# A hybrid DeltaNet and state-space layer on one Trainium2 core: values ahead of gates, the DeltaNet gate amid the state-space scan, and its branch projection in plain float32 at the scan's end

## The chip, the core and the metric

The kernel runs on one core of one Trainium2 chip. The core has a matrix engine (PE; its weight loads are shown as PEld), a vector engine (DVE), a scalar engine (ACT), a general engine (POOL) and 16 DMA engines; most DMAs are issued by SP's queue, the stores of results by ACT's. On-chip data lie in SBUF; matmuls write to PSUM, eight banks in all.

The metric is device microseconds (us) of one execution. Before the change the median of three runs is 1307.09 us (1301.83 to 1307.75). The profile is of one more execution.

## The reference, cut to what matters

One layer over 256 latent tokens and 256 context tokens with 1024 channels, everything in float32: a half-step SwiGLU block, a token mixer, a second half-step SwiGLU block and a final norm. The mixer is where the change lies. It projects its normalised input `h` with one wide weight, and runs a gated DeltaNet and a Mamba-2 scan (SSD) in both directions beside each other; each branch is gated, projected to 1024 channels, scaled by a sigmoid gate, and the sum is projected once more:

```python
u = h @ w_in
qkv, za, a, beta, zb, xbc, dt, gates = jnp.split(u, ...)
qkv = jax.nn.silu(conv(qkv, gdn_conv_w))          # q, k, v: 8 heads of 128
...
a_mat = jnp.where(strict, jnp.einsum('bnhid,bnhjd->bnhij', kb, k) * decay, 0.0) + jnp.eye(CHUNK)
sol = lax.linalg.triangular_solve(a_mat, rhs, left_side=True, lower=True, unit_diagonal=True)
...
ya = rmsnorm(o, gdn_norm_g) * jax.nn.silu(za)
yb = rmsnorm((y + mb_d * xs) * jax.nn.silu(zb), mb_norm_g)
merged = jax.nn.sigmoid(ga) * (ya @ w_branch_gdn) + jax.nn.sigmoid(gb) * (yb @ w_branch_mb)
return merged @ w_out
```

Here `o` is the DeltaNet's output, `y` the scan's, `ga` and `gb` the two halves of `gates`.

## The kernel before

**Tiling.** Activations stand channel-major: 128 channels on the partitions, tokens along the row, 256 for the latents alone or 512 with the context. A weight comes in units of 128 by 1024 (512 KB), one DMA each on SP's queue into one of four `raw` slots.

**Two kinds of projection.** `unit` (line 185) splits a weight into a rounded high part `whi` (ACT, line 197) and a rest `wlo` (DVE, line 201); `mm3` then runs three matmuls per block, high by high, high by low and low by high (lines 212 to 214). So go keys, values, queries, x and both branch projections. `whole` (line 634) leaves the weight as it is, and the matmul takes plain float32: so go the gates `wg` and the DeltaNet's `zA` (both line 648), and the scan's `zB` (line 1161).

**What sets the order.** The mixer's parts are generators or functions, and the string `PLAN` calls them in turn: `13/dts` sets a priority and emits `dts`, `g5` takes five steps of the gates' generator. A scheduler then orders each engine's instructions from priorities, data and free buffers by a simulated time line. So a shift in `PLAN`, or in who asks for a buffer first, moves instructions on all engines, and from then on each engine runs its list in that order.

**Keys to first merge.** `keys` (line 943) takes key heads through convolution, norm and transposes, and stores each head's Gram matrix (`pg`, line 960) to DRAM (`Gsd`); every two heads the blocks come back as `N` (line 969) in another layout. `dts` (line 870) makes the scan's step sizes and their cumulated sums `gc`, transposes these (`prow`, line 914) and stores them as `asd`. `elim` (line 1041) inverts all 32 by 32 blocks at once, on DVE, in 30 dependent steps, stores them (`Tsd`, `Ttd`), and `merge` (line 1187) loads them for one pair of token tiles and joins them with small matmuls (`pTw`, line 1242, first). Beside all this PE runs values (`values`, line 1071: projection, convolution `cv` at lines 665 to 672 on ACT and DVE, transposes `ptm`, store `vsc`), gates and queries.

**The DeltaNet chain and the scan.** After the merges, `chain_step` walks the token tiles; `gdn_norm` (line 1373) leaves `o` token-major and normalised. The scan goes by quarters (two groups of two halves). For each, `ssd_off` (line 1437) loads `xlat` and multiplies it into `yg` (line 1451), runs `pyo` and adds it (lines 1467, 1468), and `ssd_diag` (line 1471) builds two decay matrices `Es` for every token tile on DVE (lines 1499, 1507, 1510, 1512), multiplies them with x on PE (`pyd`, line 1515) and adds that (line 1516). `ssd_gate` and `ssd_norm` (lines 1518, 1527) multiply by the gate `zt`, which zB's units have stored, and scale.

**The scan's end.** `gdn_out` (line 1386) transposes `o` to channels (`pya`), multiplies by norm gain and gate (`ya`, line 1401), splits the result (`yaH` on ACT, `yaL` on POOL) and projects it with `wbg`. `ssd_out` (line 1559), for each of the two groups, transposes `yg` into PSUM (`pyb`, line 1570), one bank, and splits it (`ybH`, `ybL`, lines 1574, 1575). `mb_out` (line 1578) projects that with `wbm` (16 units), adds the branches, and projects the sum. The pools that matter: 16 slots `s4` of 4 KB per partition, shared by `yg`, `xlat`, `yaH`, `yaL`, `ybH`, `ybL`; PSUM tags `mm` (2 banks), `ch` (2), `mg` (2), `tr` (1), `sd` (1).

Of the kernel before, what the change touches and what calls it, by code (L numbers as in the profile page):

```python
# [27 lines left out]
TAGS = dict(tA=4, tS=3, tL=2, tM=2, tZ=2)  # L28
T4 = 2
NCV = 2  # L30
PLAN = """10/k3 block_decay k6 18/g5 13/dts 20/v2 g3 row_scale 5/elim 20/g7 v7 21/gdn_rows 13/m0 14/m1 13/chain_start s0 s1 m2 m3 22/q9
    B_part 27/x17 25/lat_h 22/C_part 30/g17 chain_out 13/s2 s3 14/gdn_norm 15/ssd_pre 30/zB1 zA9 zB4 15/h40 51/y0 gdn_out y1 70/mb_out"""
NG = 5
GQ = 0
EST = ("t4", "tt")
# [2 lines left out]
OSQ, YAL = "c4", "gggg"  # L38
# [30 lines left out]
ZT = ("mm", "ch")  # L69
# [67 lines left out]
class Kernel:  # L137
# [537 lines left out]
    def mixer(self, hg):  # L675
# [194 lines left out]
    def dts(self):  # L870

        nc, V = self.nc, self.nc.vector
        C = self.const
        mm = nc.tensor.matmul
        x = self.t2([P, 4, 64], "dtx", tag="tZ")
        e = self.t2([P, 4, 64], "dte", tag="tZ")
        z2 = self.t2([P, 4, 64], "dtz", tag="tL")
        V.tensor_copy(x, self.xdt)
        dt = self.dt = self.xdt
        self.softplus(dt, e, z2, x)  # L880
        g = self.t2([P, 4, 64], "dtg", tag="tL")
        V.tensor_tensor(g, dt, self.alog[:, 16:80].rearrange("p (o c) -> p o c", o=1).to_broadcast([P, 4, 64]), op=ALU.mult)
        pc = self.smp([P, 2, 4, 64], "pcd", "mg")
        for d, tri in enumerate((self.UT, self.LT)):
            mm(pc[:, 0, :, 32 * d:32 * d + 32], tri, g[:, :, 32 * d:32 * d + 32], start=True, stop=True)
        mm(pc[:, 1], self.ones, g, start=True, stop=True)
        gc = self.gc = C([P, 4, 64], "gc")
        V.tensor_copy(gc, pc[:, 0])

        gt = pc[:, 1]  # L890
        wc = self.wc = C([P, 2, 2, 32], "wc")
        for j in range(2):
            for d in range(2):
                t = 2 + j
                cs = slice(32 * d, 32 * d + 32)
                w = wc[:, j, d]
                V.tensor_tensor(w, gt[:, t, cs], gc[:, t, cs], op=ALU.subtract)
                if d == j:
                    V.tensor_tensor(w, w, gt[:, 5 - t, cs], op=ALU.add)
        nc.scalar.activation(wc, wc, AF.Exp)  # L900
        wf = wc.rearrange("p a b c -> p a (b c)")
        V.tensor_tensor(wf, wf, dt[:, 2:4], op=ALU.mult)

        wl, egm = self.wl, self.egm = C([P, 2, 32], "wl"), C([P, 2, 32], "egm")
        for d in range(2):
            cs = slice(32 * d, 32 * d + 32)
            V.tensor_tensor(wl[:, d], gt[:, d, cs], gc[:, d, cs], op=ALU.subtract)
            V.tensor_copy(egm[:, d], gt[:, d, cs])
        nc.scalar.activation(wl, wl, AF.Exp)
        nc.scalar.activation(egm, egm, AF.Exp)  # L910
        for d in range(2):
            V.tensor_tensor(wl[:, d], wl[:, d], dt[:, d, 32 * d:32 * d + 32], op=ALU.mult)
        pr = self.smp([P, P], "prow", "mg")
        nc.tensor.transpose(pr, gc[:, 0:2].rearrange("p t c -> p (t c)"), self.ident)
        rw = self.t2([P, P], "rows_a", tag="tL")
        nc.scalar.activation(rw, pr, AF.Copy, scale=-1.0)
        nc.scalar.dma_start(self.asd, rw)
# [465 lines left out]
        for t in range(2):  # L1383
            V.tensor_tensor(o[t], o[t], bc(rs[:, t], 8, P), op=ALU.mult)

    def gdn_out(self):

        nc, V = self.nc, self.nc.vector
        o, bc = self.o, self.bc
        yH = Ks(self, 8, NL, "yaH")  # L1390
        yL = Ks(self, 8, NL, "yaL")
        for h2 in range(4):
            pv = self.smp([P, 2, NL], "pya", "ch")
            for j in range(2):
# [6 lines left out]
            V.scalar_tensor_tensor(out=ya, in0=pv, scalar=self.gng, in1=zA, op0=ALU.mult, op1=ALU.mult)
            nc.scalar.copy(yH.t[j][:, hs], ya)
            (V if YAL[h2] == "v" else nc.gpsimd).tensor_tensor(yL.t[j][:, hs], ya, yH.t[j].bitcast(F32)[:, hs], op=ALU.subtract)
# [155 lines left out]
    def ssd_out(self, gi):  # L1559

        nc, V = self.nc, self.nc.vector
        y = [self.yx[gi, hf][0] for hf in range(2)]
        yH = Ks(self, 8, NL, f"ybH{gi}")
        yL = Ks(self, 8, NL, f"ybL{gi}")
        for c2 in range(4):
            pv = self.smp([P, 2, NL], "pyb", "tr")
            for j in range(2):
                c = 2 * c2 + j
                for t in range(2):
                    nc.tensor.transpose(pv[:, j, t * P:t * P + P], y[c // 4][:, t, (c % 4) * P:(c % 4) * P + P], self.ident)  # L1570
            for j in range(2):
                c = 2 * c2 + j
                g = self.mbg[:, 8 * gi + c:8 * gi + c + 1]
                nc.scalar.activation(yH[c], pv[:, j], AF.Identity, scale=g)
                V.scalar_tensor_tensor(out=yL[c], in0=pv[:, j], scalar=g, in1=yH[c].bitcast(F32), op0=ALU.mult, op1=ALU.subtract)
        self.yb.append((yH, yL))
# [124 lines left out]
```

## Time and profile before

| what | us |
|---|---|
| median of three runs | 1307.09 |
| the profiled execution's own time | 1309.47 |
| its span, first to last instruction | 1307.8 |
| first block and key units, up to 459 | PE busy 454.43 of 459 |
| rest of keys, elimination, to the first merge, 459 to 612 | PE busy 134.71 of 153 |
| merges, chain, queries and x, 612 to 855 | PE busy 236.85 of 243 |
| scan, zA, zB, 855 to 991 | PE busy 134.41, DVE 105.32 of 136 |
| scan's end and first branch, 991 to 1036 | PE busy 35.42 of 45 |
| second branch, 1036 to 1082 | PE busy 45.19 of 46 |
| output projection, second block, final norm, from 1082 | PE busy 216.78 of 226 |

The stretches are cut where the work changes. "Busy" counts an engine's instructions; the granted clock (1 is full speed) says how fast PE ran them. Its mean over the span is 0.973. A row of the chain of waits gives start, length, engine and work on the chain that ended last; a group row gives line, engine, operation, tiles and shapes with a count, then busy time and mean length in ns of one, then the engine's idle time ahead of it and what ended that.

### The profile page before, as it was taken

The numbers are of one execution on the slowest core, as the hardware profiler recorded it, in microseconds if no ns is written. First come the engines' busy times: TensorE is split into PE (matmuls) and PEld (weight loads), VectorE is DVE, ScalarE is ACT, GpSimd is POOL, SyncE is SP. The second block draws the span as 40 slices with busy tenths as digits, with TensorE's granted clock in tenths as the row PEclk, the third lists the DMA queues.
The fourth block names the chain that finished last, engine by engine and source line by source line (L and its number), as shares of the span: only waits on it lengthen the run. The fifth ranks groups of instructions, "written<-read, shape, count | busy, mean of one in ns | idle before, by whom it ended". The sixth has DMA issues, their size and how long they took to land.

```text
span 1307.8 us, 21034 instructions
## 1 busy us (share of the span) xinstructions
PE 1257.8 (96%) x8042; PEld 1096.2 (84%) x8042; DVE 950.8 (73%) x1748; ACT 482.2 (37%) x919; POOL 96.7 (7%) x119
## 2 busy tenths in 40 slices
PE   9999999999999989987999999999997999999997
PEld 8888888888899878877888899868555999999997
DVE  5997686556568964897669799847896566856655
ACT  4322122212236652254323445421223445633333
POOL 1000000000010131001110211100211002000000
PEclk9999999999999999998889999999987999999998
DMA  9566467547532389648434356568645665655552
GB/s 367 183 212 206 129 221 230 192 147 238 181 123 89 105 220 232 212 145 235 108 103 117 122 177 196 175 194 286 219 168 199 193 201 182 192 192 185 186 179 79
DMA packets 138131, 239.40 MB, mean 183 GB/s; under 512 B 41072, under 2 KB 81456, under 8 KB 137904
## 3 DMA queue, kind: packets, MB, share of 16 engines
q1 hardware_dynamic: 98688, 214.32, 51.5%
q10 hardware_dynamic: 39344, 23.76, 6.1%
q8 instruction: 63, 1.03, 0.3%
q14 instruction: 36, 0.29, 0.1%
HBM read 211.72 MB, written 26.31 MB: 182 GB/s over the span
## 4 chain that ended last, share of the span: by engine, by line
PE 65%; issue 16%; DVE 9%; DMA 8%; ACT 1%; SPq 0%; POOL 0%; ACTq 0%; DVEq 0%; POOLq 0%
PE acc L213 16%; PE acc L212 16%; PE acc L214 16%; PE acc L648 4%; DVE Es L1499 1%; PE pSs L1125 1%; PE acc L1161 1%; PE pada L318 1%; DMA raw<-in_wgs 1%; DVE Es L1510 1%; DVE wlo L201 1%; PE pn L1339 1%; DMA zsc<-zbt 1%; PE pP L1330 1%; DMA Lm<-Gsd 1%
## 5 line engine op out<-in xcount | busy, mean ns | idle before, releaser
L197 ACT CAST whi<-raw 128x1024 fp32r<-128x1024 f32 (+1 forms) x208 | 214.5, 1034 | 460.3 <-PE acc L213 350.8
L213 PE MATMUL acc<-hL,whi 128*128 128x512 f32 (+1 forms) x976 | 346.1, 355 | 0.5 <-DVE hL L468 0.5
L214 PE MATMUL acc<-hH,wlo 128*128 128x512 f32 (+1 forms) x976 | 346.5, 355 | 0.0
L212 PE MATMUL acc<-hH,whi 128*128 128x512 f32 (+1 forms) x976 | 342.4, 357 | 0.8 <-ACT cv L665 0.5
L201 DVE TENSOR_TENSOR wlo<-raw,whi 128x1024 fp32r<-128x1024 f32 (+1 forms) x208 | 249.7, 1202 | 80.0 <-ACT whi L197 78.8
L212 PEld LDWEIGHTS acc<-hH,whi 128*128 128x128 f32 x976 | 187.7, 193 | 24.6 <-ACT cv L665 0.7
L213 PEld LDWEIGHTS acc<-hL,whi 128*128 128x128 f32 x976 | 188.1, 193 | 23.9 <-DVE hL L468 0.9
L214 PEld LDWEIGHTS acc<-hH,wlo 128*128 128x128 f32 x976 | 188.0, 193 | 23.4
L290 DVE CUSTOM_DVE_ANT_0 junk<-wadat,cs 128x1024 f32<-128x1024 f32 x80 | 97.7, 1221 | 44.1 <-DMA wadat<-in_wadaT 43.4
L213 PE MATMUL acc<-aL,whi 128*128 128x256 f32 (+1 forms) x384 | 122.9, 323 | 0.0
L214 PE MATMUL acc<-aH,wlo 128*128 128x256 f32 (+1 forms) x384 | 122.3, 323 | 0.0
L212 PE MATMUL acc<-aH,whi 128*128 128x256 f32 (+1 forms) x384 | 122.2, 323 | 0.0
L667 DVE SCALAR_TENSOR_TENSOR cv<-cbuf,cc,cv 128x512 f32<-128x512 f32 (+1 forms) x144 | 97.5, 688 | 16.8 <-ACT cv L665 15.4
L648 PE MATMUL acc<-hF,raw 128*128 128x256 f32 x416 | 97.2, 390 | 7.0 <-ACT gth L1183 7.0
L648 PEld LDWEIGHTS acc<-hF,raw 128*128 128x128 f32 x416 | 80.7, 197 | 21.0 <-ACT gth L1183 7.6
L213 PEld LDWEIGHTS acc<-aL,whi 128*128 128x128 f32 x384 | 73.0, 190 | 5.6
L214 PEld LDWEIGHTS acc<-aH,wlo 128*128 128x128 f32 x384 | 72.7, 190 | 5.6
L212 PEld LDWEIGHTS acc<-aH,whi 128*128 128x128 f32 x384 | 72.6, 190 | 5.7
L604 DVE SCALAR_TENSOR_TENSOR xl<-acc,hg,xl 128x256 f32<-128x256 f32 x64 | 30.3, 481 | 47.6 <-PE acc L214 47.0
L1161 PE MATMUL acc<-raw,hF 128*128 128x512 f32 x128 | 58.6, 610 | 0.0
L1161 PEld LDWEIGHTS acc<-raw,hF 128*128 128x128 f32 x128 | 24.9, 197 | 30.0 <-issue 29.9
L401 POOL TENSOR_TENSOR sqa<-sqa,sqb 128x256 f32<-128x256 f32 x12 | 11.7, 978 | 454.9 <-ACT sqb L399 451.9
(403 smaller groups left out, 1968.4 us busy)
## 6 DMA issues: line engine op xcount, KB each, us to landing
raw<-in_wgu SPq DMA_DIRECT2D x76, 512.0 KB, 4.2
wadat<-in_wadaT SPq DMA_DIRECT2D x56, 512.0 KB, 4.1
raw<-in_wdn SPq DMA_DIRECT2D x44, 512.0 KB, 3.8
wada<-in_wada SPq DMA_DIRECT2D x16, 512.0 KB, 9.6
raw<-in_wg SPq DMA_DIRECT2D x16, 512.0 KB, 3.7
Es<-asd SPq DMA_DIRECT2D x16, 512.0 KB, 4.7
raw<-in_wxs SPq DMA_DIRECT2D x16, 512.0 KB, 4.3
raw<-in_wzB SPq DMA_DIRECT2D x16, 512.0 KB, 3.8
```

The costliest lines, as they stand in the source:

```text
L197: nc.scalar.copy(hi, raw)
L201: engs[i % len(engs)].tensor_tensor(lo[:, c:c + w], raw[:, c:c + w], hi[:, c:c + w].bitcast(F32), op=ALU.subtract)
L212: mm(acc, wh, xh, start=start, stop=False)
L213: mm(acc, wh, xl, start=False, stop=False)
L214: mm(acc, wl, xh, start=False, stop=stop)
L290: self.nc.vector.tensor_tensor_reduce(out=self.junk, in0=w, in1=self.cs[s], scale=1.0, scalar=0.0, op0=ALU.mult, op1=ALU.add, accum_out=out)
L318: mm = lambda c, q: nc.tensor.matmul(pa[:, c], loads[k][c][:, q * P:q * P + P], self.cTs[:, q:q + 1].to_broadcast([P, P // 2, 2]), start=q ...
L604: nc.vector.scalar_tensor_tensor(out=xs, in0=acc[:, NL * s - g0:NL * s - g0 + NL], scalar=hg[s][:, m:m + 1], in1=xs, op0=ALU.mult, op1=ALU ...
L648: self.nc.tensor.matmul(acc, w[:, k * P:k * P + P], self.hF[:, k], start=k == 0, stop=k == KD - 1)
L667: nc.vector.scalar_tensor_tensor(out=u3, in0=buf[:, 0:R, j:j + 64], scalar=cw[:, j:j + 1], in1=u3, op0=ALU.mult, op1=ALU.add)
L1125: nc.tensor.matmul(pS[:, d], self.Btok[:, j, m // 8], w[:, d, j], start=j == 0, stop=j == 1)
L1161: nc.tensor.matmul(accs[t], self.hF[:, k, sl], w[:, wsl], start=k == 0, stop=k == 7)
```

## The change

Four edits, beside what the scheduler makes of them.

1. In `PLAN`, three values stand where five gates stood, two gates follow behind `dts`, and the rest of the gates go ahead of the rest of the values behind the elimination.
2. `dts` loses its last four statements, which become `dts_rows` and are called behind `gdn_rows`.
3. `gdn_out` is cut in two. `gdn_pre` (transposes, gate, now into one plain float32 tile set `ya`) is called behind the last zA unit, ahead of the scan's loop and of the zB units. `gdn_out`, the projection, is called behind both `ssd_out`; its weights are taken whole, in plain float32, so no split of `ya` and none of `wbg` is left. Its accumulators alternate between two PSUM tags.
4. `pyb` alternates between the banks `tr` and `sd`.

```diff
-PLAN = """10/k3 block_decay k6 18/g5 13/dts 20/v2 g3 row_scale 5/elim 20/g7 v7 21/gdn_rows 13/m0 14/m1 ...
-    ... 15/ssd_pre 30/zB1 zA9 zB4 15/h40 51/y0 gdn_out y1 70/mb_out"""
+PLAN = """10/k3 block_decay k6 18/v3 13/dts 18/g2 20/v2 g3 row_scale 5/elim 20/g10 v4 21/gdn_rows dts_rows 13/m0 14/m1 ...
+    ... 15/ssd_pre 30/zB1 zA9 29/gdn_pre 30/zB4 15/h40 51/y0 y1 60/gdn_out 70/mb_out"""
...
+    def dts_rows(self):
+
+        nc = self.nc
         pr = self.smp([P, P], "prow", "mg")
-        nc.tensor.transpose(pr, gc[:, 0:2].rearrange("p t c -> p (t c)"), self.ident)
+        nc.tensor.transpose(pr, self.gc[:, 0:2].rearrange("p t c -> p (t c)"), self.ident)
...
-    def gdn_out(self):
+    def gdn_pre(self):
...
-        yH = Ks(self, 8, NL, "yaH")
-        yL = Ks(self, 8, NL, "yaL")
+        self.ya = Ks(self, 8, NL, "ya", F32)
         for h2 in range(4):
...
-            V.scalar_tensor_tensor(out=ya, in0=pv, scalar=self.gng, in1=zA, op0=ALU.mult, op1=ALU.mult)
-            nc.scalar.copy(yH.t[j][:, hs], ya)
-            (V if YAL[h2] == "v" else nc.gpsimd).tensor_tensor(yL.t[j][:, hs], ya, yH.t[j].bitcast(F32)[:, hs], op=ALU.subtract)
+            V.scalar_tensor_tensor(out=self.ya.t[j][:, hs], in0=pv, scalar=self.gng, in1=zA, op0=ALU.mult, op1=ALU.mult)
+
+    def gdn_out(self):
...
         for m in range(8):
-            acc = self.proj("wbg", m, yH, yL, NL)
+            w = self.whole(self.I["wbg"][m])
+            acc = self.mmp([P, NL]) if ZT[m % 2] == "mm" else self.smp([P, NL], "acc", ZT[m % 2])
+            for k in range(8):
+                nc.tensor.matmul(acc, w[:, k * P:k * P + P], self.ya[k], start=k == 0, stop=k == 7)
...
-            pv = self.smp([P, 2, NL], "pyb", "tr")
+            pv = self.smp([P, 2, NL], "pyb", ("tr", "sd")[c2 % 2])
```

What the scheduler makes of it is read from each engine's list (line, operation, tiles, shape, count of like rows). First PE at the end of the keys: `pg` are Gram matrices, `l2b` and `l2t` the norm's transposes, `pcd` the sums of `dts`; L648 is a gate, 8 matmuls a unit, L212 to L214 here a value. Before, from the last but one Gram:

```order
L960 MATMUL pg<-kT 128x128 x4
L939 MATMUL l2b<-ident,l2n 128x128 x4
L925 MATMUL l2t<-ident,kcv_3441 128x128 x2
L648 MATMUL acc<-hF,raw 128x256 x9
L914 MATMUL prow<-ident,gc 128x128
L960 MATMUL pg<-kT 128x128 x4
L939 MATMUL l2b<-ident,l2n 128x128 x4
L1000 MATMUL prow<-ident,sel_3364 128x128
L648 MATMUL acc<-hF,raw 128x256 x8
```

Now, from the third Gram ahead of the last to the one before the last (line numbers are 4 higher):

```order
L648 MATMUL acc<-hF,raw 128x256 x2
L964 MATMUL pg<-kT 128x128 x4
L943 MATMUL l2b<-ident,l2n 128x128 x4
L648 MATMUL acc<-hF,raw 128x256 x6
L885 MATMUL pcd<-dtg,UT 128x4x32
L885 MATMUL pcd<-dtg,LT 128x4x32
L886 MATMUL pcd<-dtg,ones 128x256
L214 MATMUL acc<-hH_3181,wlo 128x512
L212 MATMUL acc<-hH_3181,whi 128x512
L213 MATMUL acc<-hL_3183,whi 128x512
L214 MATMUL acc<-hH_3181,wlo 128x512
L964 MATMUL pg<-kT 128x128 x4
```

Where gates filled PE between Grams, values now do: ahead of the last Gram stand 3.4 values and two gates, where there were 1.3 values and five gates. The transpose of `dts` (L914) has left this place; it follows the third gate. Further on, the first merge (`pTw`) stands behind the first query unit and a part of it, where it stood behind six: five query projections earlier.

Second, PE at the scan's end. L1161 (now L1165) is zB, L1515 (L1522) is `pyd`, L1413 the new projection. Before:

```order
L1161 MATMUL acc<-raw,hF 128x512
L1515 MATMUL pyd<-xlat,Es 128x64 x16
L1161 MATMUL acc<-raw,hF 128x512 x23
L1515 MATMUL pyd<-xlat,Es 128x64 x16
L1396 MATMUL pya<-ident,o_7186 128x128
L1396 MATMUL pya<-ident,o_7187 128x128
```

Now:

```order
L1165 MATMUL acc<-raw,hF 128x512
L1413 MATMUL acc<-ya,raw 128x256 x2
L1522 MATMUL pyd<-xlat,Es 128x64 x16
L1413 MATMUL acc<-ya,raw 128x256 x30
L1522 MATMUL pyd<-xlat,Es 128x64 x16
L1577 MATMUL pyb<-ident,yg 128x128 x32
L1413 MATMUL acc<-ya,raw 128x256 x32
L212 MATMUL acc<-ybH_8376,whi 128x256
```

The zB units are done ahead of the last two `pyd`, half of the branch projection fills the place between these, all 32 transposes of the scan's output follow, then the other half, then `mb_out` with nothing among it. The 16 `pya` transposes now stand among the last zA unit's rows.

Third, DVE in the scan's first half. `zbt` and `zth` are the gates of zB and zA, `yg<-xlat` is the product of line 1451 (now 1458). Before, ahead of the first quarter's decay matrices:

```order
L1165 SCALAR_TENSOR_TENSOR zbt<-zbt,acc 128x512 x2
L1451 TENSOR_TENSOR yg<-xlat,mbD 128x512 x2
L1467 TENSOR_TENSOR yo<-pyo,cbm 128x512
L1128 TENSOR_TENSOR sst<-pSs,egm 128x256
L1468 TENSOR_TENSOR yg<-yg,yo 128x512
L1175 SCALAR_TENSOR_TENSOR zth<-zth,acc 128x256 x2
```

Now, behind the first quarter's decay matrices:

```order
L1179 SCALAR_TENSOR_TENSOR zth<-zth,acc 128x256
L1403 SCALAR_TENSOR_TENSOR ya<-pya,cc,zA 128x512
L1458 TENSOR_TENSOR yg<-xlat,mbD 128x512 x2
L1403 SCALAR_TENSOR_TENSOR ya<-pya,cc,zA 128x512
L1475 TENSOR_TENSOR yg<-yg,yo 128x512 x3
L1474 TENSOR_TENSOR yo<-pyo,cbm 128x512
L1458 TENSOR_TENSOR yg<-xlat,mbD 128x512 x2
L1475 TENSOR_TENSOR yg<-yg,yo 128x512
```

The products of all four quarters, and the loads of `xlat` on SP's queue ahead of them, come only behind or among the four `ya`; before, they stood among the chain's end and the x units. On SP, two of the four `zA` loads now stand among zB's weights.

More of the change, by code (lines that the diff above doesn't have):

```diff
@@ L30 @@
 NCV = 2
-PLAN = """10/k3 block_decay k6 18/g5 13/dts 20/v2 g3 row_scale 5/elim 20/g7 v7 21/gdn_rows 13/m0 14/m1 13/chain_start s0 s1 m2 m3 22/q9
-    B_part 27/x17 25/lat_h 22/C_part 30/g17 chain_out 13/s2 s3 14/gdn_norm 15/ssd_pre 30/zB1 zA9 zB4 15/h40 51/y0 gdn_out y1 70/mb_out"""
+PLAN = """10/k3 block_decay k6 18/v3 13/dts 18/g2 20/v2 g3 row_scale 5/elim 20/g10 v4 21/gdn_rows dts_rows 13/m0 14/m1 13/chain_start s0 s1 m2 m3 22/q9
+    B_part 27/x17 25/lat_h 22/C_part 30/g17 chain_out 13/s2 s3 14/gdn_norm 15/ssd_pre 30/zB1 zA9 29/gdn_pre 30/zB4 15/h40 51/y0 y1 60/gdn_out 70/mb_out"""
 NG = 5
@@ L1396, in gdn_out @@
                     nc.tensor.transpose(pv[:, j, t * P:t * P + P], o[t][:, 2 * h2 + j], self.ident)
-            ya = self.t2([P, 2, NL], "ya")
             j, hs = h2 // 2, slice(2 * (h2 % 2), 2 * (h2 % 2) + 2)
@@ L1400, in gdn_out @@
             nc.sync.dma_start(zA, self.zAsc[2 * h2:2 * h2 + 2].rearrange("m p n -> p m n"))
-            V.scalar_tensor_tensor(out=ya, in0=pv, scalar=self.gng, in1=zA, op0=ALU.mult, op1=ALU.mult)
-            nc.scalar.copy(yH.t[j][:, hs], ya)
-            (V if YAL[h2] == "v" else nc.gpsimd).tensor_tensor(yL.t[j][:, hs], ya, yH.t[j].bitcast(F32)[:, hs], op=ALU.subtract)
+            V.scalar_tensor_tensor(out=self.ya.t[j][:, hs], in0=pv, scalar=self.gng, in1=zA, op0=ALU.mult, op1=ALU.mult)
+    def gdn_out(self):
+        nc, V = self.nc, self.nc.vector
         mg = self.mg = Ks(self, 8, NL, "mg", F32)
         for m in range(8):
-            acc = self.proj("wbg", m, yH, yL, NL)
+            w = self.whole(self.I["wbg"][m])
+            acc = self.mmp([P, NL]) if ZT[m % 2] == "mm" else self.smp([P, NL], "acc", ZT[m % 2])
+            for k in range(8):
+                nc.tensor.matmul(acc, w[:, k * P:k * P + P], self.ya[k], start=k == 0, stop=k == 7)
             ga = self.t2([P, NL], "ga", tag="tL")
```

## The prediction

> **What bounds the kernel now.** I read the page's busy shares first, then the table by stretches of the span, then the chain of waits in the stretches that the change touches.
>
> ```profile
> PE 1257.8 (96%) x8042; PEld 1096.2 (84%) x8042; DVE 950.8 (73%) x1748; ACT 482.2 (37%) x919; POOL 96.7 (7%) x119
> 455.00:480.00 25.00, 25.00 (x156) 22.72 (x155) 20.08 (x44) 15.08 (x52) 12.72 (x19) 1.00 0.68 178
> 480.00:492.00 12.00, 6.35 (x19) 4.95 (x18) 4.58 (x7) 3.13 (x8) 0.40 (x2) 0.72 0.97 275
> 492.00:514.00 22.00, 22.00 (x113) 18.96 (x112) 7.02 (x8) 5.82 (x15) 4.03 (x3) 1.00 1.06 208
> 514.00:585.00 71.00, 68.05 (x338) 58.34 (x336) 63.48 (x106) 28.10 (x56) 0.00 (x0) 1.00 0.57 179
> 585.00:612.00 27.00, 17.31 (x128) 16.50 (x129) 18.74 (x36) 14.34 (x32) 2.46 (x2) 0.86 0.96 277
> 612.00:855.00 243.00, 236.85 (x2078) 208.93 (x2077) 199.60 (x411) 98.14 (x221) 30.90 (x38) 0.95 0.48 145
> 916.00:991.00 75.00, 73.41 (x249) 41.66 (x247) 68.93 (x150) 23.61 (x51) 12.39 (x7) 0.95 0.61 206
> 991.00:1015.00 24.00, 14.42 (x87) 12.75 (x86) 13.21 (x26) 8.21 (x17) 6.03 (x5) 0.72 0.46 147
> 1015.00:1036.00 21.00, 21.00 (x179) 21.00 (x177) 13.90 (x19) 9.21 (x13) 0.00 (x0) 1.00 0.72 226
> ```
>
> Columns of the stretches are length, then busy time of PE, its weight loads, DVE, ACT and POOL, then granted clock, DMA share and GB/s. PE is the bound: only its holes can be won. There are three where the change works. In 480 to 492 it stands for 5.65 us at a clock of 0.72, with the DMA share at 0.97. In 585 to 612 it stands for 9.7 us at 0.86. In 991 to 1015 it stands for 9.6 us at 0.72. From 916 to 991 DVE is nearly as full as PE (68.93 of 75): there PE's time is not all that counts.
>
> The chain of waits (start, length, engine, work) names what ends the first two holes:
>
> ```profile
> 479.29 6.18 DMA raw<-in_wg
> ...
> 501.44 0.91 PE pg L960 x8
> ...
> 506.96 6.62 DMA N<-Gsd
> 522.39 20.72 PE acc L648 x96
> 583.37 0.97 DVE D L1058
> 590.77 5.51 DMA ch<-ksc
> 596.30 4.28 DMA TT<-Tsd
> 611.79 2.58 PE pTw L1242 x48
> ```
>
> Hole one ends with a late weight of a gate (raw<-in_wg), while the key chain (Grams pg, their store and reload into N, then the elimination) ends only behind it. Hole two is the tail from the elimination's last copies at 584 to the first merge, pTw, at 611.8.
>
> **The change part by part.**
>
> *Values ahead of gates.* A gate unit is 16 records of L648; 96 of them took 20.72 us, 0.216 each, so 3.45 us of PE per 512 KB weight. A value unit is 24 split matmuls of 512 columns, the shape that alone fills this stretch (PE busy, count, clock, DMA share, GB/s):
>
> ```profile
> 320.00:340.00 20.00, 20.00 (x90) 1.00 0.71 245
> ```
>
> That is 0.222 each, 5.3 us per 512 KB. Ahead of the last Gram, before has five gates and 1.3 values (24.1 us), the new order 3.4 values and two gates (24.9 us). So PE has as much to do there, but draws one weight less, in the stretch whose DMA share is at 0.97. From 459.4, where the key units end, to the last Gram at 502.4 PE was busy for 20.6 + 6.35 + 10.4 = 37.3 us, 2 of it lost at half clock: with 0.8 more to do it needs 36. I take hole one as mostly closed, so that Gram comes at 495, 7 us earlier. The bounds are 0 (the key chain itself, not the weight, sets the Gram) and 7.
>
> The bigger part is DVE's load while the elimination runs:
>
> ```profile
> L667 DVE SCALAR_TENSOR_TENSOR cv<-cbuf,cc,cv 128x512 f32<-128x512 f32 x24 | 17.5, 741 | 0.0
> L1052 DVE TENSOR_TENSOR N<-N,etmp 128x60 f32<-128x60 f32 (+14 forms) x30 | 15.0, 501 | 0.7
> L1049 DVE TENSOR_TENSOR etmp<-N 128x60 f32<-128x60 f32 (+14 forms) x30 | 15.0, 499 | 3.0 <-DMA vsc<-vt 2.4
> L201 DVE TENSOR_TENSOR wlo<-raw,whi 128x1024 fp32r<-128x1024 f32 x10 | 12.2, 1218 | 3.6 <-ACT whi L197 3.5
> L672 DVE SCALAR_TENSOR_TENSOR cv<-cv 128x512 f32<-128x512 f32 x5 | 3.4, 682 | 0.0
> ```
>
> These are DVE's groups from 514 to 585. The elimination is 30 us of steps and about 4.4 of scaling and copies; five values' convolutions take 17.5 + 3.4 = 20.9 us (4.2 each), and ten splits of weights 12.2. In the new order gates, which need neither, stand behind the fourth and fifth value; I count two convolutions (8.4) and three splits (3.7) beside the elimination. 34.4 + 8.4 + 3.7 = 46.5, with the same 7.5 us of waits 54 us in place of 71. Starting 7 us earlier as well, the elimination ends at 561 in place of 585.
>
> The first merge however also stands five query projections earlier on PE (24 split matmuls of 256 columns each, 179 records in 21 us in the stretch 1015 to 1036, 0.117 each, so 2.8 us each and some 15 in all with a begun one). Before had done the same work at 596.4 (611.8 less 15.4). So the gain is 596.4 minus the new time of pTw. With before's whole tail behind the elimination (26.4 us from 585.4 to 611.8) that is 587, with a tail of 15 us, since that tail held ACT and DVE work of values now done, 576: a gain of 9 to 20. PE itself, without any hole, arrives at about 574: from 459.4 to 611.8 it was busy for 20.6 + 6.35 + 22.0 + 68.05 + 17.3 = 134.3 us; less 15.4, and less 5 at half clock, 114 remain. I take **-15 us**, with bounds of +5 (below, the rival with DVE ahead of the keys) and -25 (all holes and the clock's loss up to 612). Behind pTw, PE is packed (236.85 of 243), so a lead survives the stretch to 855; what is late next is the merges' own wait, pTw behind DVE.
>
> *The transposed rows of dts.* Store and transpose move by some tens of us; their reader, the Es load of the scan, issues hundreds of us later. Nothing, in both directions.
>
> *The scan's end.* Before, this ran after the last pyd (991.3):
>
> ```profile
> 991.34 4.48 DMA zsc<-zbt
> 995.88 2.68 DMA zt<-zsc
> 1002.96 0.76 DVE ya L1401
> 1004.51 1.52 POOL yaL L1403
> 997.00:1003.00 6.00, 1.08 (x4) 0.71 (x4) 2.53 (x7) 2.34 (x7) 0.71 (x1) 0.52 0.46 139
> 1003.00:1009.00 6.00, 4.46 (x19) 4.17 (x20) 5.41 (x9) 2.33 (x4) 2.42 (x2) 0.50 0.30 89
> ```
>
> The third hole is this chain, then the projection at half clock. The change takes ya, yaH and yaL out of it, and puts the z units ahead of the last pyd. For that the projection costs more PE: plain F32 at 3.45 us a unit is 27.6 us for eight, split at 24 x 0.12 = 2.88 is 23.0: **+4.6 us**. DVE's eight splits of it (1.22 each) and ACT's casts go; they lay beside PE's 23 us, so only the three splits ahead of the last pyd count, below.
>
> ```profile
> L648 PE MATMUL acc<-hF,raw x416: 377/379/796, 459.3 to 924.5; 128*128 128x256 f32 x139
> ```
>
> The trace's row of that line (durations, then its first and last start) counts 416 records for 26 units, 16 each, where the program has 8: a plain F32 matmul runs as two. The Trainium skill speaks against the change here: the page "FP8 and Floating Point Precision", section "TensorE Precision Notes", gives true FP32 four passes through the array; against three for the split, that is an estimate of 4/3 x 23.0 = 30.7 us, +7.7 in place of +4.6, and the whole sum would be 3 us less of a gain. The trace has 2 x 0.216 to 0.117 for one split pass, a ratio of 3.7, so it agrees nearly.
>
> What the change defers is on DVE. The z load and ya now stand ahead of the latents' loads, and with them the yg products:
>
> ```profile
> L1451 DVE TENSOR_TENSOR yg<-xlat,mbD 128x512 f32<-128x512 f32 x8 | 5.1, 683 | 7.6 <-DMA xlat<-xsc 7.6
> 918.30 3.81 DVE Es L1499 x8
> L1468 DVE TENSOR_TENSOR yg<-yg,yo 128x512 f32<-128x512 f32 x10 | 6.8, 682 | 0.1
> L1467 DVE TENSOR_TENSOR yo<-pyo,cbm 128x512 f32<-128x512 f32 x9 | 6.1, 677 | 0.0
> ```
>
> Before, the eight L1451 lay at 790 to 916, where DVE has room, and the second quarter's first Es row was at 918.3. zA's last records started at 924.5; with the pyd that stood among them now behind, and pya ahead of their end, the first ya falls at some 918. From it to that Es row DVE has 4 ya at 0.75, 8 L1451, 7 L1468, 3 L1467, 2 L1516, a gate and a z row: 18 us, so Es starts at 936 to 938. (No other engine's work covers this: if DVE had room for the yg products earlier, it would be nothing.) What is left of 68.93 without three splits and a few z rows is 63.7: the last pyd falls at 1002 to 1008. PE reaches it at about the same time: 991.3 + 1.8 for the sixteen pya (0.44 for four transposes, by the pyb row below) + 13.8 for the four projections put ahead of it, less 3 of lost clock. I take 1004.
>
> From there: the gate, norm and transposes. The two DMAs above (7.2 us) now lie ahead. What remains of the chain is four rows of 0.68 (two L1516, two gates), four scales and, as an estimate, 1.8 for the squares and the root between them: 7.8, and 3 for the last two transposed sets on the two banks (an estimate from their four passes of 256 columns): 10.8. PE does 3.4 of transposes meanwhile; the four other projections stand behind all 32 of them: 13.8, and 2.5 lost at half clock, as after the third hole (4.46 us of work at 0.50). The last branch's projection starts at 1031, where it started at 1033, with transposes pyb among it and three waits for their one bank (7.1 us, of which some 3 fall behind 1033): an even start of 1036. That is -5. Counted by PE's work alone (108.8 us from 916 to 1036, less 5 at half clock, plus 4.6, with 7.4 idle and 2.5 slow) it is 1034, -2. I take **-4**, bounds -10 and +12.
>
> ```profile
> L1536 DVE TENSOR_SCALAR yg<-yg,yr 128x512 f32<-128x512 f32 x4 | 3.3, 887 | 0.0
> PE pyb L1570 <- DVE ybL L1575: 7.1, 3, 4.5
> 1032.60 0.44 PE pyb L1570 x4
> ```
>
> **Sum.** -15 - 4 = -19. The profiled run took 1309.47 us (span 1307.8), 2.4 above the median of the three, 1307.09; half of that taken off as well gives 1289.
>
> **The rivals.**
>
> *Early gain kept, scan's end gives back.* DVE's deferral of 20 us is not caught up, since 916 to 991 has only 6 us of DVE free: last pyd at 1008 to 1012, the late part at 0 to +4: 1292 to 1301. For it: 68.93 of 75. Against: PE is as late there anyhow.
>
> *The hole only moves.* The tail behind the elimination is DMA (590.77 to 600.58 in the chain, the share 0.96), and the first merge asks earlier for the same loads: then pTw comes at 594 or later, and only the late 4 us stay: 1302 to 1306, no change. Against: the longest wait of PE in that hole is not for a DMA but for a value's convolution.
>
> ```profile
> PE ptm L1066 <- DVE cv L672: 4.4, 1, 4.4
> ```
>
> *Slower.* The scan's end turns wholly DVE-bound: the deferral of 20 us stands, and each of the last two quarters waits once more for its Es rows, which queue on SP behind the z weights (4.7 us from issue to landing): last pyd at 991.3 + 20 + 9.4 = 1021, the last projection at 1048, +12 on the even start. It decides from the point where the early gain is under 5.5; it would be, if the values' convolutions (3.4 of them, 14.3 us of DVE ahead of N, where 1.3 and 5.5 us stood) outrun the key chain: N 7 us later, not earlier, pTw at 601, +5 to 0. Then 1316 to 1325.
>
> ```profile
> Es<-asd SPq DMA_DIRECT2D x16, 512.0 KB, 4.7
> ```
>
> *More.* The tail is short and PE packed: early -22, late -9: 1267 to 1280.
>
> **How the numbers follow.** Forecast (1281 to 1297) 0.50; scan's end gives back 0.20; the hole moves 0.12; slower 0.08; more 0.10. About 0.5% (6.5 us) is what a measurement of this kernel tells from no change. Faster by more, below 1300.6: 0.50 + 0.15 + 0.10 = 0.75; within, 0.05 + 0.12 = 0.17; slower 0.08. The range of 8 in 10 leaves out half of the last case, half of the hole that moves and the slower one: 1270 to 1304.
>
> **What would show it.** Early: PE over 95% busy from 480 to 492, the last pg at 495 or before, the elimination's copies at 555 to 565, pTw at 570 to 587, and its successors up to 855 by 15 us earlier. Late: ya near 920 less the lead, the second quarter's first Es 18 to 20 us behind ya's start, last pyd 13 us later relative to the lead, then one PE hole of about 7 us, and L1413, the new projection's line, at 3.45 us a unit. The early part is wrong if pTw waits for DMA at 590 or later; the late part, if DVE has holes before the last Es row, or the last projection starts later than 1036 less the lead.

## The result, and the profile after

| | median us | runs | ratio to before (95%) |
|---|---|---|---|
| before | 1305.22 (1301.83 to 1310.19) | 8 | |
| changed | 1297.26 (1291.65 to 1298.57) | 8 | 0.9923 (0.9903 to 0.9943) |

The change makes the kernel faster by 0.8%: 8 us by the medians, 10 by the ratio. The new time lies in the range of 1270 to 1304, just above the forecast's own 1281 to 1297, and the gain is about half of the 19 us that the sum gave. The two profiled executions differ by more, 1307.8 to 1295.8 us of span, since that of before was a long one: its 1309.47 us stand near the top of its runs, 4 above their median. So gains are taken from the runs, and places in time from the profiles, with that excess in mind.

The page of the changed kernel, its line of busy times, then the table by stretches at the cuts used before (length, busy time of PE, its weight loads, DVE, ACT, POOL; granted clock, DMA share, GB/s):

```profile
PE 1254.7 (97%) x7978; PEld 1090.9 (84%) x7978; DVE 943.2 (73%) x1740; ACT 470.9 (36%) x907; POOL 94.7 (7%) x115
```

```profile
480.00:492.00 12.00, 12.00 (x69) 10.60 (x68) 10.27 (x27) 5.37 (x15) 1.94 (x3) 1.00 0.92 233
492.00:514.00 22.00, 20.98 (x108) 17.76 (x107) 10.26 (x14) 7.00 (x18) 0.31 (x1) 1.00 0.75 185
514.00:585.00 71.00, 67.47 (x471) 58.80 (x469) 59.71 (x102) 23.16 (x50) 5.38 (x4) 0.98 0.77 245
585.00:612.00 27.00, 25.80 (x262) 24.30 (x260) 24.70 (x54) 11.56 (x25) 3.22 (x8) 0.87 0.69 186
612.00:855.00 243.00, 235.36 (x1851) 203.16 (x1851) 191.59 (x391) 100.09 (x227) 30.09 (x30) 0.99 0.47 145
896.00:912.00 16.00, 12.68 (x50) 7.24 (x49) 8.03 (x14) 0.98 (x2) 0.00 (x0) 0.95 0.68 216
916.00:991.00 75.00, 71.40 (x261) 43.39 (x259) 68.48 (x152) 20.75 (x49) 11.33 (x7) 0.98 0.63 217
992.00:1007.00 15.00, 8.56 (x36) 6.71 (x36) 9.82 (x23) 7.26 (x18) 0.71 (x1) 0.50 0.06 17
1007.00:1024.00 17.00, 16.75 (x65) 14.33 (x66) 6.19 (x12) 3.51 (x4) 0.00 (x0) 0.83 0.53 168
```

Hole one is gone (12.00 of 12), hole two almost (25.80 of 27, at 0.87 where the clock was 0.86), and from 612 to 855 the clock is 0.99 where it was 0.95, which the prediction had not counted. There is a new hole at 896 to 912, where both PE and DVE wait, and the third one has moved: 15 us at half clock behind the last `pyd`.

The chain of waits shows the early part done sooner (start, length, engine, work):

```profile
492.04 0.91 PE pg L964 x8
493.58 5.63 DMA Gsd<-kb
505.27 2.36 DVE N L1049 x2
514.87 9.10 DMA vsc<-vt
573.05 3.80 DMA TT<-Ttd
```

The last Gram is at 492 (before 501.4), N at 505 (before 514). The first `pTw` starts at 572.1 where it started at 610.9. At the scan's end it shows

```profile
896.81 6.11 DMA xlat<-xsc
903.36 3.64 DMA zA<-zAsc
907.09 0.75 DVE ya L1403
975.34 3.81 DVE Es L1506 x8
989.19 3.65 PE pyd L1522 x16
992.84 1.91 PE pyb L1577 x8
1007.25 16.80 PE acc L1413 x64
```

that the last `pyd` ends at 992.8. Before it ended at 991.3, so the lead of the early part is gone at this point. What is left of the gain comes behind it: 303 us from there to the end, where it was 316.5.

### The profile page after: what moved, and what is told of

Same layout as the page of the kernel before. It is cut to its first block, busy times and chain, and to the rows that moved or that the text cites. A ratio compares the mean times of both kernels' runs of the same rounds, so it can differ in the third digit from the quotient of the medians.

```text
span 1295.8 us, 20862 instructions
## 1 busy us (share of the span) xinstructions
PE 1254.7 (97%) x7978; PEld 1090.9 (84%) x7978; DVE 943.2 (73%) x1740; ACT 470.9 (36%) x907; POOL 94.7 (7%) x115
## 4 chain that ended last, share of the span: by engine, by line
PE 70%; issue 15%; DVE 7%; DMA 6%; ACT 1%; SPq 1%; POOL 0%; DVEq 0%; POOLq 0%; ACTq 0%
PE acc L213 16%; PE acc L212 16%; PE acc L214 16%; PE acc L1165 4%; PE acc L648 3%; PE acc L1413 2%; PE pn L1343 1%; PE pyd L1522 1%; PE pSs L1129 1%; PE pada L318 1%; DVE N L1056 1%; DVE etmp L1053 1%; DMA raw<-in_wgs 1%; DVE wlo L201 1%; DMA gr<-gsd 1%
## 5 line engine op out<-in xcount | busy, mean ns | idle before, releaser
L197 ACT CAST whi<-raw 128x1024 fp32r<-128x1024 f32 (+1 forms) x200 | 206.2, 1033 | 456.6 <-PE acc L213 369.0
L214 PE MATMUL acc<-hH,wlo 128*128 128x512 f32 (+1 forms) x976 | 344.9, 354 | 0.0
L212 PE MATMUL acc<-hH,whi 128*128 128x512 f32 (+1 forms) x976 | 340.8, 356 | 0.9 <-ACT cv L665 0.5
L201 DVE TENSOR_TENSOR wlo<-raw,whi 128x1024 fp32r<-128x1024 f32 (+1 forms) x200 | 240.1, 1202 | 79.1 <-ACT whi L197 77.1
L212 PEld LDWEIGHTS acc<-hH,whi 128*128 128x128 f32 x976 | 186.7, 192 | 24.7 <-ACT cv L665 1.1
L214 PEld LDWEIGHTS acc<-hH,wlo 128*128 128x128 f32 x976 | 186.8, 191 | 23.5
L214 PE MATMUL acc<-aH,wlo 128*128 128x256 f32 (+1 forms) x384 | 122.3, 323 | 0.0
L212 PE MATMUL acc<-aH,whi 128*128 128x256 f32 (+1 forms) x384 | 122.2, 323 | 0.0
L648 PE MATMUL acc<-hF,raw 128*128 128x256 f32 x416 | 93.0, 379 | 1.9 <-DMA raw<-in_wg 1.9
L648 PEld LDWEIGHTS acc<-hF,raw 128*128 128x128 f32 x416 | 78.0, 190 | 14.9 <-ACT gth L1187 2.5
L212 PEld LDWEIGHTS acc<-aH,whi 128*128 128x128 f32 x384 | 72.6, 190 | 5.7
L214 PEld LDWEIGHTS acc<-aH,wlo 128*128 128x128 f32 x384 | 72.7, 190 | 5.5
L1165 PE MATMUL acc<-raw,hF 128*128 128x512 f32 x128 | 57.8, 601 | 0.7 <-DVE ya L1403 0.7
L1165 PEld LDWEIGHTS acc<-raw,hF 128*128 128x128 f32 x128 | 24.2, 192 | 29.7 <-issue 28.7
```

Source lines behind the costliest of these rows:

```text
L197: nc.scalar.copy(hi, raw)
L201: engs[i % len(engs)].tensor_tensor(lo[:, c:c + w], raw[:, c:c + w], hi[:, c:c + w].bitcast(F32), op=ALU.subtract)
L212: mm(acc, wh, xh, start=start, stop=False)
L214: mm(acc, wl, xh, start=False, stop=stop)
L648: self.nc.tensor.matmul(acc, w[:, k * P:k * P + P], self.hF[:, k], start=k == 0, stop=k == KD - 1)
L1165: nc.tensor.matmul(accs[t], self.hF[:, k, sl], w[:, wsl], start=k == 0, stop=k == 7)
```

## The experiments

Two theories stood at the start. **A**: the early part is worth about 20 us (by count of matmuls, the work done at 855 in the profile of before is done at 835 in the changed kernel), and the scan's end gives back about half. **B**: the early part is worth what was measured, and the scan's end nothing. Each kernel below was timed in five rounds beside before; ratios are to before, gains are worked out from the ratio and the median of before in that set (1304.2 to 1304.9 us).

| kernel | ratio (95%) | gain, us |
|---|---|---|
| e1_early | 0.9877 (0.9863 to 0.9891) | 16.0 |
| e2_late | 1.0026 (1.0012 to 1.0041) | -3.4 |
| e4_early_banks | 0.9860 (0.9844 to 0.9875) | 18.3 |
| e5_ya_c4 | 0.9827 (0.9814 to 0.9840) | 22.6 |
| e6_split_proj | 0.9940 (0.9919 to 0.9962) | 7.8 |
| e7_gates_first | 1.0017 (0.9997 to 1.0037) | -2.2 |
| e8_values_beside | 0.9900 (0.9879 to 0.9921) | 13.0 |
| e9_dts_whole | 0.9884 (0.9857 to 0.9910) | 15.1 |
| e10_late_c4 | 0.9956 (0.9939 to 0.9973) | 5.7 |
| e11_nb7 | 0.9979 (0.9965 to 0.9993) | 2.7 |
| e12_c4_nb7 | 0.9908 (0.9895 to 0.9922) | 12.0 |

**The early edits alone** (e1_early): the new `PLAN` up to `dts_rows`, the rest of before.

> Only the early edits (values ahead of gates, the rows of dts behind gdn_rows); the scan's end as before. Theory A (the early part gains about 20 us, since the same PE work that stood done at 855 before stands done at 835 in the changed kernel, and the scan's end gives about 9 of it back): 16 to 20 us faster than before, 8 to 12 faster than the changed kernel. Theory B (the early part gains only the 8 us that the whole change gained, and the scan's end is neutral): 6 to 10 faster than before, equal to the changed kernel.

16.0 us faster: A, at its lower end. The 20 had been read from the long execution of before. Against the changed kernel it is 6 us by the ratios and 8.5 by the medians, at or under the lower end of the expectation. **The late edits alone** (e2_late): the old early part, and `gdn_pre`, `gdn_out` and the banks of the change.

> Only the late edits (gdn_pre amid the scan, plain float32 projection at the end, two banks); the early part as before. Theory A: 6 to 11 us slower than before, the second quarter's first Es row about 20 us behind ya's start. Theory B: within 3 us of before. The prediction on record had this part at 4 us faster.

3.4 us slower, between the two theories' numbers, but on the other side of zero from the 4 us of gain on record. The second quarter's first Es row starts 27.4 us behind the first `ya` (906.9 to 934.3), where 20 was expected. The sum of both, 12.6 us of gain, is a little more than the changed kernel's 10.

The profiled spans of e2_late and before, 1304.6 and 1307.8, say the opposite of the runs. That is the long execution of before: PE's list is the same in both beyond the last `pTw`, and yet that stands 6.0 us earlier in e2_late (first before, then e2_late; the last number of a row's times is the start of its last instruction):

```profile
L1242 PE MATMUL pTw<-TB,Lm x256: 185/191/258, 610.9 to 720.5; 32*32 32x32 f32 x128
L1242 PE MATMUL pTw<-TB,Lm x256: 184/191/257, 608.4 to 714.5; 32*32 32x32 f32 x128
```

Counted from that point the profiles agree with the runs. Starts of the last `pTw` and the last `pyd`, and the ends of the spans, for the kernels that follow as well:

| kernel | last pTw | last pyd | end | pTw to pyd | pyd to end |
|---|---|---|---|---|---|
| before | 720.5 | 991.1 | 1307.8 | 270.6 | 316.7 |
| e2_late | 714.5 | 1002.6 | 1304.6 | 288.1 | 302.0 |
| e10_late_c4 | 715.0 | 988.9 | 1296.8 | 273.9 | 307.9 |
| e1_early | 672.1 | 971.1 | 1288.6 | 299.0 | 317.5 |
| changed | 669.0 | 992.4 | 1295.8 | 323.4 | 303.4 |
| e5_ya_c4 | 670.1 | 973.9 | 1280.3 | 303.8 | 306.4 |

Alone, the late edits put the last `pyd` 17.5 us later and shorten what follows it by 14.7; on top of the early edits it is 24.4 and 14.1.

**Why the scan's end pays** (e5_ya_c4). `ya` takes two of the sixteen rotating `s4` slots ahead of the scan, and with that the `yg` and `xlat` tiles come two slots later in the rotation. The two `c4` slots, of the same size, are idle there:

```diff
-        self.new = lambda: (kern.s4 if tag == "s4" else kern.tt)([P, w, n], name, dt)
+        self.new = lambda: getattr(kern, tag)([P, w, n], name, dt)
...
-        self.ya = Ks(self, 8, NL, "ya", F32)
+        self.ya = Ks(self, 8, NL, "ya", F32, tag="c4")
```

> The changed kernel, with ya's two tiles taken from the two c4 slots, which are idle in the scan, in place of two s4 slots, so that yg and xlat of all quarters come as early as before. Theory A1 (what the scan's end gives back is the deferral of the yg products and of the xlat loads, by the slots that ya takes): 8 to 12 us faster than the changed kernel, last pyd by 10 earlier. Theory A2 (it is the float32 projection, 4.6 us more PE, and the transposes ahead of it): within 3 us of the changed kernel.

22.6 us faster than before and 12.6 faster than the changed kernel, a little more than expected, with the last `pyd` 18.5 earlier (10 expected): the deferral through the slots is the cause, and this is the fastest kernel of all. The instructions of line 1458 (`yg`) are back beside the x units. Some rows of DVE's timeline, first the changed kernel, from the first `ya` to the second quarter's first decay row, then this one:

```profile
894.66 0.75 DVE L1403 SCALAR_TENSOR_TENSOR ya<-pya,cc,zA 128x512 f32<-128x512 f32 x1 [1.33 <-PE pya L1399]
902.94 1.29 DVE L1458 TENSOR_TENSOR yg<-xlat,mbD 128x512 f32<-128x512 f32 x2 [3.52 <-DMA xlat<-xsc]
907.09 0.75 DVE L1403 SCALAR_TENSOR_TENSOR ya<-pya,cc,zA 128x512 f32<-128x512 f32 x1 [2.85 <-DMA zA<-zAsc]
918.16 1.28 DVE L1458 TENSOR_TENSOR yg<-xlat,mbD 128x512 f32<-128x512 f32 x2
922.26 2.18 DVE L1506 SCALAR_TENSOR_TENSOR Es<-Es,gc 128x128 f32<-128x128 f32 x8
```

```profile
897.62 3.83 DVE L1506 SCALAR_TENSOR_TENSOR Es<-Es,gc 128x128 f32<-128x128 f32 x8 [2.24 <-POOL Es L1504]
910.90 0.74 DVE L1403 SCALAR_TENSOR_TENSOR ya<-pya,cc,zA 128x512 f32<-128x512 f32 x1
```

The Es row starts at 897.6 in place of 922.3; with the early edits alone it starts at 899.8. And the table by stretches of this kernel shows what the plain float32 projection is good for, once DVE is not late:

```profile
974.00:993.00 19.00, 17.24 (x95) 15.10 (x94) 9.23 (x21) 6.91 (x17) 0.71 (x1) 1.00 0.61 201
993.00:1008.00 15.00, 14.03 (x67) 12.27 (x65) 6.97 (x13) 4.72 (x7) 0.00 (x0) 1.00 0.59 191
```

From the last `pyd` at 973.9 to the start of the last projection at 1008 PE is busy for 31 of 34 us, at full clock: half of the projection stands among the transposes.

**The same without the early edits** (e10_late_c4): e2_late with `ya` in `c4`.

> Only the late edits, with ya in the c4 slots, and the early part as before. If the deferral of the yg products is what the scan's end paid (as e5_ya_c4 shows for the whole change): 5 to 9 us faster than before, 9 to 12 faster than e2_late, the same as e5_ya_c4 gains over the early edits alone. If the late part pays only where the early part has made PE early: within 3 of before.

5.7 us faster than before, 9.1 better than e2_late: the late part would have been a gain of about the size on record but for the slots, with or without the early part. From the last `pTw` to the end its profile is 5.5 us shorter than that of before (the table), which fits the 5.7.

**The two banks** (e4_early_banks): e1_early with `pyb` on `tr` and `sd` in turn.

> The early edits and the two banks for the transposes pyb, nothing else of the scan's end. If the one bank's waits (7.1 us in the profile of before, 3 of them behind the other projection) bound the end: 2 to 4 us faster than the early edits alone. If the chain behind the last pyd bounds it: within 1 us of them.

2.3 us better than e1_early. The intervals overlap, so this is the likely size and no more; it fits the 3 us of the prediction. From the last `pyd` to the end its profile has 315.1 us, where before and the five other kernels with the old scan's end have 316.1 to 318.3.

**Float32 or split** (e6_split_proj). Ahead of the projection two casts and two differences of the whole `ya` into four `s4` tiles, then `proj` as before:

```diff
+        yH = Ks(self, 8, NL, "yaH")
+        yL = Ks(self, 8, NL, "yaL")
+        for j in range(2):
+            nc.scalar.copy(yH.t[j], self.ya.t[j])
+            nc.gpsimd.tensor_tensor(yL.t[j], self.ya.t[j], yH.t[j].bitcast(F32), op=ALU.subtract)
...
-            w = self.whole(self.I["wbg"][m])
...
+            acc = self.proj("wbg", m, yH, yL, NL)
```

> The changed kernel with ya in the c4 slots (as e5_ya_c4), and the branch projection split again: two casts and two differences of ya, then three matmuls per block. If plain float32 costs what the rows gave (27.6 against 23.0 us of PE) and the end is bound by PE: 3 to 5 us faster than e5_ya_c4. If what counts is that the projection needs no casts and no splits (16 rows on ACT and DVE while DVE is full): 2 or more slower.

14.8 us slower than e5_ya_c4, the second outcome, but not for its reason: behind the last `pyd` (975.9) DVE and ACT are not full. The table by stretches of this kernel tells more:

```profile
980.00:990.00 10.00, 1.94 (x8) 1.57 (x8) 4.64 (x11) 4.12 (x11) 0.55 (x1) 0.50 0.48 171
990.00:1000.00 10.00, 5.33 (x21) 4.25 (x22) 5.36 (x12) 5.26 (x10) 3.22 (x3) 0.50 0.05 14
1000.00:1010.00 10.00, 10.00 (x65) 10.00 (x65) 2.93 (x4) 2.10 (x2) 1.62 (x1) 0.73 0.08 22
```

The projection starts only at 999, behind `yaL` on POOL (2.36 us at 996.9), so nothing fills PE among the transposes, and it then begins at half clock. The casts themselves are short (two of 1.04 us on ACT, from 995.8), but they stand late in ACT's list, among the last casts of the scan's output. With the casts right behind `ya` the split projection might have filled PE as well; no run has them there, so this one shows what a late preparation costs, and not that float32 is better. Nor does it measure the price of float32 matmuls, since their place has changed too; that price is in the rows: 12 records of L1413 in 2.66 us at 970.6, 0.222 each, 3.5 us a unit against the 3.45 counted.

**Which early edit** (e7_gates_first, e8_values_beside). The first keeps five gates ahead, then five values; the second has three values and two gates ahead, then values ahead of gates.

```diff
-18/v3 13/dts 18/g2 20/v2 g3 row_scale 5/elim 20/g10 v4
+18/g5 13/dts 20/v5 row_scale 5/elim 20/g10 v4
```

> The early edits, but with the five gates first, as before; then five values, and the rest of the gates ahead of the rest of the values. So hole one (480 to 492, gates waiting for weights) stays and the elimination gets fewer convolutions. If hole one is worth the 5.65 us and the lost clock: 4 to 8 us slower than the early edits alone, the last pg at 502. If all comes from DVE's load beside the elimination: within 2 of them.

```diff
-18/v3 13/dts 18/g2 20/v2 g3 row_scale 5/elim 20/g10 v4
+18/v3 13/dts 18/g2 row_scale 5/elim 20/v6 g13
```

> The early edits, but with values ahead of gates also behind the row scale: three values and two gates first, then six values and only then gates. Hole one is filled, the convolutions stand beside the elimination as before. If DVE's load there (some 17 us) sets the first merge: 8 to 14 us slower than the early edits alone, the elimination's copies at 570 to 580. If it doesn't: within 2 of them.

With gates first nothing is left of the gain: 2.2 us slower than before, 18 slower than e1_early, where 4 to 8 was expected. Hole one is open again (PE busy for 7.60 of the 12 us), with the last Gram at 498.8. With three values ahead 13.0 of 16.0 us stay in e8_values_beside. So the three values ahead of the keys' end carry the early part, and the order behind the elimination is worth some 3 us, between the two expectations; the intervals just overlap. The first merge comes 11.4 us later there than in e1_early (585.1 against 573.7), but the last `pyd` at the same time (971.2 and 971.1): PE had done more of the values meanwhile. In e7_gates_first some rows of DVE's timeline show what the five values do when they come late:

```profile
511.45 2.36 DVE L1049 TENSOR_TENSOR N<-N,D 128x1024 f32<-128x1024 f32 x2 [3.53 <-DMA N<-Gsd]
515.16 7.72 DVE L667 SCALAR_TENSOR_TENSOR cv<-cbuf,cc,cv 128x512 f32<-128x512 f32 x6
523.41 1.53 DVE L667 SCALAR_TENSOR_TENSOR cv<-cbuf,cc,cv 128x512 f32<-128x512 f32 x2
528.90 3.11 DVE L667 SCALAR_TENSOR_TENSOR cv<-cbuf,cc,cv 128x512 f32<-128x512 f32 x4 [2.57 <-ACT cv L665]
533.32 0.25 DVE L1053 TENSOR_TENSOR etmp<-N 128x60 f32<-128x60 f32 x1
```

N was ready at 514, and the elimination's first step stood behind convolutions until 533. The expectation that it gets fewer of them was wrong. The convolutions' time on DVE around the elimination, up to its copies, is (table by stretches, rows that write or read `cv`; length, then PE, PEld, DVE, ACT, clock, DMA share, GB/s), for before, the changed kernel, e7_gates_first and e8_values_beside in this order:

```profile
505.00:586.00 81.00, 3.43 (x24) 2.86 (x24) 23.78 (x34) 9.40 (x14) 1.00 0.64 182
```

```profile
505.00:560.00 55.00, 1.31 (x8) 0.84 (x8) 5.71 (x8) 1.67 (x3) 1.00 0.76 250
```

```profile
511.00:597.00 86.00, 4.56 (x30) 3.38 (x30) 31.09 (x44) 10.01 (x17) 1.00 0.58 184
```

```profile
504.00:559.00 55.00, 1.23 (x8) 1.05 (x9) 18.95 (x22) 5.30 (x8) 1.00 0.52 163
```

The first window starts 9 us ahead of N, which is scaled from 514.2; the others start with it. From 514 to 585 before has 20.9 us of convolutions (the prediction's rows). 31.1 us go with the longest stretch (86 us), 5.7 with one of the two shortest (55). But 18.95 go with 55 too, where 570 to 580 was expected for the copies and 559 came. So convolutions alone don't set its length: splits of weights take 12.2 us of DVE in e7_gates_first and 12.9 in before's window, but 4.19 in the changed kernel's and 1.22 in that of e8_values_beside, which also has none of the changed kernel's wait for a value's store (`vsc<-vt`, 4.2 us of DVE's idle time).

**Hole one** (e11_nb7). SP's timeline of before shows that it stood at the reload of N for the second Gram pair, with the gates' weights behind it:

```profile
467.70 0.33 SPq L191 DMA_DIRECT2D raw<-in_wv  x1
476.28 1.38 SPq L969 DMA_DIRECT2D N<-Gsd  x2
477.76 1.44 SPq L191 DMA_DIRECT2D raw<-in_wv  x1
479.29 7.89 SPq L638 DMA_DIRECT2D raw<-in_wg  x3
```

The kernel before, with one reload behind the last Gram (`NB = (7,)` for `(1, 3, 5, 7)`), leaves PE's list as it is:

> The kernel before, with N reloaded once, behind the last Gram, in place of four times behind every second one; PE's list is the same. Theory C (hole one is SP's queue, which stood at N's reload from 468 to 476 while the gates' weights stood behind it): PE busy 10 or more of the 12 us from 480 to 492, the last pg 4 to 8 us earlier, 3 to 10 us faster than before, unless the one larger reload of N comes later than before's last. Theory D (hole one is DMA throughput, share 0.97): the hole stays, within 2 us of before.

```profile
480.00:492.00 12.00, 10.96 (x56) 9.33 (x55) 4.83 (x9) 4.30 (x16) 1.79 (x3) 1.00 1.07 341
```

```profile
L960 PE MATMUL pg<-kT x64: 270/275/275, 447.8 to 494.2; 128*128 128x128 f32 x64
```

The hole is filled while the DMA share is higher than before (1.07 against 0.97), and the last Gram starts at 494.2 in place of 502.1: theory C, the queue, and not D, although the gain is just under the 3 us that C gave. Yet N is scaled at 512.9 (before 514.2), as the one reload is late, and the gain is 2.7 us. So a filled hole one alone is worth little, as long as N and the elimination hardly come earlier. **On top of the best kernel** (e12_c4_nb7) the single reload only does harm:

> The changed kernel with ya in the c4 slots and N reloaded once. In the changed kernel SP stands at N's reload as long (17.6 us in the table of waits), but PE has values ahead of it. If that cover holds already: within 2 us of e5_ya_c4. If weights are still late somewhere: 2 to 5 faster.

10.6 us slower than e5_ya_c4, which neither expectation had. There hole one has cover already (PE busy for 12.00 of the 12 us in both; SP's wait of 17.6 us, 29.0 in before, costs PE nothing there), and N comes at 509.0 in place of 506.1, `pTw` at 578.6 in place of 572.6. That is 6 us; at the last `pyd` it is 7.6 (981.5 and 973.9), and the cause of the rest is open.

**The rows of dts** (e9_dts_whole): e1_early with `dts` in one piece.

> The early edits of the plan with dts in one piece, as before: its transpose and store stand ahead of the row scale. All theories: within 1.5 us of the early edits alone; a larger difference would say that the rows of dts stood in the way of the key chain on PE or ACT.

15.1 against 16.0 us: no difference clear of noise.

## Why the prediction came out as it did

**Early, -15: the size was right.** e1_early gives 16.0. The steps read in the changed kernel's trace: the last Gram at 492 (forecast 495), the elimination's copies end at 559.5 (561), DVE busy for 46.4 us in that stretch (46.5), `pTw` at 572 (570 to 587). But two reasons behind the sizes need mending. Hole one was put down to weights that come late where the DMA share is 0.97; e11_nb7 shows that it was SP's queue at N's reload, and that its 5.65 us by themselves aren't the gain. And the sentence that gates behind the fourth and fifth value are "the bigger part" gave the credit to the wrong half of the plan: by e8_values_beside that order is worth some 3 us of 16, the values ahead of the Gram the rest. The sum of DVE's rows came out all the same: fewer convolutions (5.7 us for 8.4) and more of other rows than counted, and 8.6 us of waits for 7.5.

**Late, -4: wrong in sign.** Alone it costs 3.4 us, on top of the early edits 6 (16.0 less 10). The prediction saw the deferral of the `yg` products and priced it; the step that failed is "the last pyd falls at 1002 to 1008", 13 us later than before. Counted from the last `pTw` it is 17.5 later alone and 24.4 on top of the early edits. (In e2_late's profile it does end at 1002.9, but in an execution that stood 6.0 ahead of before's by then.) Two terms were too small.

First, from the first `ya` to the second quarter's first Es row 18 to 20 us were counted, as DVE work alone. It is 27.6 (894.66 to 922.26), and 27.4 in e2_late. DVE was busy for only 8 of the 16 us from 896 to 912. SP's rows stand in this order: the first `xlat` at 896.8, then the fourth `zA` load, which waited until 903.4, and only then, from 904.3, the other three quarters' `xlat` loads. SP's waits from 890 to 912 say that the `zA` loads stood for the store of the gates that they read:

```profile
SPq L1402 <- DMA zAsc<-zth: 7.7, 2, 6.0
```

The sum had added up DVE's rows, and no wait for the loads that feed them. In e2_late the first `ya` came earlier than the 918 counted (906.9, or 912.9 with those 6.0), which hid more than half of this.

Second, "PE reaches it at about the same time" left no room for DVE being the bound. From 980 to 990 of the changed kernel PE was busy for 6.4 of 10 us, DVE for 9.86; the last quarter's decay matrices set the end:

```profile
980.00:990.00 10.00, 6.40 (x37) 5.55 (x36) 9.86 (x26) 1.78 (x3) 0.00 (x0) 0.94 0.42 147
```

Behind the last `pyd` 27 us were counted to the start of the last projection, and 31.6 came (992.8 to 1024.4; 30 in e2_late): the chain took 14.4 in place of 10.8. Most of the missing 3.6 is PE's clock. It had fallen to 0.50, so eight transposes took 1.95 us where they take 0.87 in e5_ya_c4 at full clock, and three such sets stand in the chain. That half-clock time was priced for the projection alone and forgotten for the transposes ahead of it. The projection's half itself was right: 64 records in 16.80 us, where 16.3 was the sum.

For the late edits alone that is some 4.5 us at the last `pyd` and 3 behind it: 7.5, the way from -4 to +3.4. That the new time still lies in the range is no merit of the late part: the range was wide enough to hold its wrong sign.

**The rivals.** "Early gain kept, scan's end gives back" is what happened: its late part of 0 to +4 holds the 3.4 of e2_late, its last `pyd` 17 to 21 later the 17.5, its 1292 to 1301 the 1297.3. It had a chance of 0.20, the forecast with both gains 0.50. The argument against it, that PE is as late there anyhow, was the one that failed. "The hole only moves" is out by `pTw` at 572, and "slower" by the early gain of 16, as it asked for less than 5.5. "More" (1267 to 1280) did not come either; e5_ya_c4, with its median of 1281.9, is near it, but it is another kernel.

**What was priced at nothing** stayed so: the rows of `dts`. The 4.6 us of float32 were rightly sized per unit (3.5 us), but in e5_ya_c4 they buy a projection that needs no casts and none of the `s4` slots, and half of it runs among the transposes.

## What to carry to other kernels

When a tile is made earlier, ask which pool it takes its slot from: in a rotating pool it pushes back every tile that is allocated after it, also those that have nothing to do with it. When a bound engine's deferred work is added up, add the loads that feed it and what stands ahead of them on their queue, and where a sum takes PE's clock as halved behind a hole, as these traces show it from 992 to 1007 (0.50), take it so for all of the work there, the transposes too, and not for the last piece alone. And a matmul that needs no preparation can be worth more than its cost in PE time where it fills the holes of a chain, as in e5_ya_c4.

## What the runs showed that was not expected

The DMA share says little of whether weights are late because of throughput: hole one stood at a share of 0.97 and 275 GB/s, and with N's reload moved out of the way the same 12 us went at 1.07 and 341 GB/s with PE nearly full. The clock also counted beside the holes: from 612 to 855 PE's busy time in the changed kernel is within 1.5 us of that before (235.36 and 236.85), while the mean clock rose from 0.95 to 0.99. Across all traces it is 0.95 to 0.97 there in the five kernels whose first merge comes at 608 or later, and 0.96 to 0.99 in the eight where it comes at 570 to 585. How many us of the early gain are the clock's isn't shown: before and e2_late, with the same list for PE there but for the last 40 us, already differ by 0.95 and 0.97.
